# Later row-number conversion, gathered products at 0.9 a block, later gate turning and query sums in one region, in a decoder layer on one Trainium2 core

## The chip, the cores and the metric

The kernel runs on one core of a Trainium2 chip. Five engines work side by side, each through its own list of instructions in order: TensorE (PE: matmuls and transposes), VectorE (DVE), ScalarE (ACT), GpSimd (POOL) and SyncE (SP). SP issues the direct loads, POOL the indirect ones (gathers) and small copies; 16 DMA engines carry them. The metric is the device time of one execution in microseconds; lower is better.

## The reference, cut to what matters

One decoder layer for 256 tokens of width 2048: a mixing part (attention and retention, not touched here) and then a retrieval of experts. For each token and each of 8 heads, 16 of 16384 experts are chosen by two-part keys; each expert is one row of `w_u` and one row of `w_v`.

```python
q = (hf @ w_q).reshape(T, PEER_HEADS, 2, PEER_QUERY_DIM // 2)
s_half = jnp.einsum('thpd,hpkd->thpk', q, sub_keys)
v_half, i_half = lax.top_k(s_half, K)                       # K = 16
cand_s = (v_half[:, :, 0, :, None] + v_half[:, :, 1, None, :]).reshape(T, PEER_HEADS, K * K)
cand_i = (i_half[:, :, 0, :, None] * PEER_N_KEYS + i_half[:, :, 1, None, :]).reshape(T, PEER_HEADS, K * K)
top_s, pick = lax.top_k(cand_s, K)
experts = jnp.take_along_axis(cand_i, pick, axis=-1)
gates = jax.nn.softmax(top_s, axis=-1)
...
a = jnp.einsum('cd,ced->ce', hc, w_u[ec])
coef = gc * jax.nn.gelu(a)
return jnp.einsum('ce,ced->cd', coef, w_v[ec])
```

All of it is float32.

## The kernel before, in words

After the mixing part come the **queries**: 16 chunks of `wq`, each a sum over 16 blocks of the input (`t_block`, L232 to L246) into a PSUM tile `psA`. Both operands are split into a high and a low fp32r part, and three products are summed: high by high, high by low, low by high. `psA` has two regions of 256 columns; per block one matmul of 512 columns writes both, one of 256 adds to the second, and `summed` (L249 to L252) adds the regions with a copy on ACT and an addition on DVE.

Then the experts are worked through in **four stages** of 64 blocks each. In the two u stages (`u_half`, called u0 and u1) a block is one 1-MB load of `in_u` on SP and 16 fp32 matmuls (two rows each in the trace, `psU<-xT,raw`) that give the inner products of 128 experts with the dense tokens; in the two v stages (`v_group`, v0 and v1) a block is one 1-MB load of `in_v` and 20 matmuls into `acc`. Loads go into a ring of eight buffers (`set_ring`).

Dense are only 192 of the 256 tokens (TD). The other tokens' experts, and some rows of the last dense ones, are fetched one by one: 176 **gathered products**, each an indirect DMA of 128 rows of 8 KB (1.05 MB) that POOL issues (`gather`, L834) and one DVE instruction over 128x2048 (L942 or L948). They are of four kinds in this order: 32 "m", 64 "u", 16 "o", 64 "v". Up to four gathers are issued ahead of their products (`fetch`, `most`). The row numbers that a gather reads come from the top-k: `rows_of` and `rows_of_o` lay them out by small DMAs on POOL (`sx`, `sm_`, and by way of `dro` the tile `smo`), and two DVE instructions convert them to integers (`off`, `offm`). `STEPS` lists the blocks of v0, u1 and v1 that take a product; in u0 a rule does it (below).

The **gates** of u0's dense tokens are computed inside u0, for each half of the tokens (tt = 1 first, then 0): `cands` and eight `pick` (top-k; three of tt = 1 are done earlier), `gates` (subtract the maximum, for tt = 1 also start and convert the row numbers), `gates_exp` (ACT), `gates_norm` (DVE), `gates_turned` (PE: two transposes into the tile `ptr`, first of the expert numbers `ex`, then of the gates `gt`), `gates_by_slots` (DVE). After both come 24 groups in turn: `g_make` (DVE builds one-hot sets `o`, `o2m`), `g_sum` (PE, tile `pg`), `g_put` (DVE).

Where these stand between the blocks is **planned** when the program is built: `u_half` keeps two estimated clocks, `pe[0]` (a block costs PASS: 4.36 us in u0, 3.93 in u1) and `dve[0]` (each step has a cost: `cands` 4.0, a `pick` 3.9, a product 2.4 to 2.7), and places a step when its engine's clock allows. A transposition is placed once `pe[0]` has reached the chain's `ready` + 4. A product is placed from the third block after the first `fetch`, one a block, while DVE isn't too far ahead. A group's sum is placed once `pe[0]` has passed the estimated end of its one-hots, and only one set may be ahead of the sums. From block 3 on, the order so planned is the program order on PE, DVE and ACT (`fixed`, `pin`). `later` holds steps that `tick()` runs one per block. In u1, when the last "u" product is placed, `o_rows` issues the DMA that brings `h2o` back for the "o" products, and no product is placed for two blocks (`hold`).

Of the kernel before, what the change touches and what calls it, by code (L numbers as in the profile page):

```python
# [20 lines left out]
P = 128  # L21
# [21 lines left out]

STEPS = dict(u0=[j for j in range(6, HALF - 6) if j % 8 != 1], v0=[j for j in range(HALF - 6) if j % 5 != 4],
             u1=[j for j in range(HALF - 10) if j % 5 != 1])

# [4 lines left out]
TUS = (TU, TU - NO)  # L51
PASS = (4.36, 3.93)
NL = 3

# [65 lines left out]
def body(ctx, tc, a, out, dbg=None, stop=None):  # L120
# [112 lines left out]
    def t_blocks(pool, src_chunks, tags=("A", "A"), parts=2, dst=None):  # L233

        if dst:
            split_to(load(src_chunks[0]), *dst, parts)
        w = [dst] if dst else [split(load(c), parts=parts) for c in src_chunks]
        ps = [pool.tile([P, 2, S], F32, name="psA", tag=t) for _, t in zip(w, tags)]
        for k in range(KB):
            sl = slice(k * P, (k + 1) * P)  # L240
            for p_, (hi, lo) in zip(ps, w):
                nc.tensor.matmul(p_, hi[:, sl], act[:, k], start=k == 0, stop=False, skip_group_check=True)  # L242
                nc.tensor.matmul(p_[:, 1, :], lo[:, sl], hh[:, k, :], start=False, stop=k == KB - 1, skip_group_check=True)  # L243
        return ps

    def t_block(pool, src_chunk, tag="A", **kw):  # L246
        return t_blocks(pool, [src_chunk], (tag,), **kw)[0]

    def summed(ps, dst, n=S):  # L249

        nc.scalar.copy(dst, ps[:, 1, 0:n])
        nc.vector.tensor_add(dst, dst, ps[:, 0, 0:n])  # L252

# [498 lines left out]
    with ExitStack() as gctx:  # L752
# [541 lines left out]
        for i in range(16):  # L1294
            ps = first[i] if i < 2 else t_block(up, wq(i), qbank(i), dst=early if i == 2 else None)
            q = tk.tile([P, S], F32, name="pq", bufs=3)
            summed(ps, q)
            pend.append((i, q))
            if i < KB - LATE:
                ada_chunk(5, LATE + i, crow2)  # L1300
            if 4 <= i < 8:
                rows_in(i - 4)
            if i > 1:
                scores(*pend.pop(0))
            if i == 10:
                cands(1, 0, 4)
            elif i in EARLY:
                pick(1, EARLY.index(i))
# [27 lines left out]
        def gates(tt):  # L1336
# [6 lines left out]
            if tt == 1:  # L1343
                vec.tensor_copy(off, sx[:, 0, :])
                vec.tensor_copy(offm, sm_[:, 0, :])
                rows_of_o(0, ex)
                at_[0] = True

# [52 lines left out]
        def u_half(pool, hf, s2):  # L1401
# [4 lines left out]
            pe = [0.0]  # L1406
            dve = [0.0 if hf else 18.0]
            chains = [] if hf else [chain(1), chain(0)]
# [3 lines left out]
            for j in range(HALF):  # L1412
# [6 lines left out]
                def run(c, kinds):  # L1419
                    while c and c[0][0] in kinds:  # L1420
# [8 lines left out]
                        else:  # L1429
                            if pe[0] < c.ready + 4:  # L1430
                                return
# [11 lines left out]
                if summed_ and summed_[0][0] < j:  # L1443
# [3 lines left out]
                    dve[0] += 0.1 + 0.012 * j  # L1447
                if made and made[0][0] < pe[0]:
                    _, q, o = made.pop(0)
                    summed_.append((j, q, g_sum(pool, *o)))  # L1450
                    end += 0.5
# [3 lines left out]
                nxt = order[0] if order else None  # L1455
                if not any(chains) and nxt is not None and not made and dve[0] < end and (not hf or TD // 8 - len(order) < 1 + 0.45 * j):
                    if not oh:
# [25 lines left out]
                else:  # L1483
                    if at_[0] and not gone:
                        gone = j
                        fetch()
                    go = gone and j >= gone + 3 and dve[0] < end + (8 if any(chains) else 2) and j < HALF - 5
                if go and left[0]:
                    sparse(1)
                    dve[0] += 2.7 if any(chains) else 2.4  # L1490
# [60 lines left out]
```

## Time and profile before

| | us |
|---|---|
| median of 3 runs (lowest, highest) | 1874.88 (1872.93, 1877.63) |
| profiled execution, its own time | 1876.13 |
| its span | 1874.4 |
| PE busy | 1781.3 (95%) |
| DVE busy | 1532.1 (82%) |
| matmuls of u0 and u1 (`psU`) | 551.3 |
| queries, from about | 566 to 665 |
| u0, from about | 660 to 993 |
| v0, from about | 993 to 1286 |
| u1, from about | 1286 to 1561 |

Busy is the time in which an engine executes; PE is busy nearly throughout, so its few idle stretches and what ends them are what to look for. In the rows of a timeline, "[7.36 <-DVE gt L818]" says that the engine sat idle 7.36 us before the instruction, until DVE's write of `gt` released it. L818 is the line of a helper through which all planned instructions of DVE, ACT and PE are recorded, so those rows are told apart by their tiles. `sm__5028` is `sm_` or its integer copy, `s`, `raw` and `rows` as outputs of L834 are the buffers that gathers fill.

### The profile page before, as it was taken

Reading aid. Unit: us, or ns where it says so; the run is one execution under the profiler, and the core shown is the slowest. Engines: PE = TensorE matmul, PEld = TensorE weight load, DVE = VectorE, ACT = ScalarE, POOL = GpSimd, SP = SyncE. Lnnn points to the kernel's source line nnn. Section 1 sums busy time; section 2 is a strip of 40 time slices with the busy share of each in tenths; the row PEclk is TensorE's granted clock in tenths of the full one; section 3 lists DMA queues with packets and bytes.
Section 4 is the critical chain, followed back from the end, with each engine's and each line's share of the span. In section 5 each row is a group of like instructions: output and inputs, shape, how many; then the busy total and the mean of one; then the engine's idle time right before and its main releaser. Section 6 shows DMA issues by size and latency. Waiting matters only on the chain.

```text
span 1874.4 us, 28635 instructions
## 1 busy us (share of the span) xinstructions
PE 1781.3 (95%) x11296; PEld 1558.8 (83%) x11296; DVE 1532.1 (82%) x2378; ACT 707.9 (38%) x1281; POOL 425.2 (23%) x289
## 2 busy tenths in 40 slices
PE   5899999999889998979999999999899999999996
PEld 4899888798668898979998777778899998777774
DVE  7988889899689996679978999974667736999887
ACT  3444454645344421011124554552111114555554
POOL 1000001011010023222213544421323214444310
PEclk9999899999899999989999999999899999999998
DMA  8989888889788779999998999998999989999993
GB/s 345 404 324 374 299 299 306 341 301 343 286 318 298 268 258 332 419 426 424 425 387 342 414 417 415 406 330 365 409 426 426 426 366 363 420 420 418 392 333 97
DMA packets 97496, 673.00 MB, mean 359 GB/s; under 512 B 11905, under 2 KB 12177, under 8 KB 19025
## 3 DMA queue, kind: packets, MB, share of 16 engines
q1 hardware_dynamic: 66818, 467.78, 64.3%
q0 software_dynamic: 30544, 203.40, 26.8%
q8 instruction: 89, 1.46, 0.3%
q14 instruction: 45, 0.37, 0.0%
HBM read 662.81 MB, written 5.41 MB: 357 GB/s over the span
## 4 chain that ended last, share of the span: by engine, by line
PE 76%; DMA 10%; DVE 9%; issue 3%; ACT 1%; POOL 1%; SPq 0%; POOLq 0%; ACTq 0%; DVEq 0%
PE acc L1090 30%; PE psU L818 21%; PE psN L458 7%; PE psA L242 3%; PE bkB L359 2%; PE psD L359 2%; DMA raw<-in_adaT 2%; DMA rows<-in_urow,sm__5028 2%; DVE wlo L162 2%; DVE raw L202 2%; PE psA L243 2%; PE pg L818 1%; PE bkC L359 1%; PE bvB L411 1%; DMA raw<-in_v 1%
## 5 line engine op out<-in xcount | busy, mean ns | idle before, releaser
L818 PE MATMUL psU<-xT,raw 128*128 128x160 f32 (+1 forms) x4096 | 551.3, 296 | 0.0
L818 PEld LDWEIGHTS psU<-xT,raw 128*128 128x128 f32 x4096 | 540.0, 192 | 0.2
L1090 PE MATMUL acc<-whi,cc 128*128 128x512 f32 x1512 | 369.4, 391 | 0.0
L1067 DVE TENSOR_TENSOR wlo<-raw,whi 128x2048 fp32r<-128x2048 f32 x126 | 287.9, 2285 | 67.5 <-issue 50.9
L1090 PEld LDWEIGHTS acc<-whi,cc 128*128 128x128 f32 x1512 | 283.9, 188 | 70.3 <-issue 1.9
L1090 PE MATMUL acc<-wlo,cc 128*128 128x512 f32 x1008 | 253.8, 392 | 0.0
L1064 ACT CAST whi<-raw 128x2048 fp32r<-128x2048 f32 x126 | 240.8, 1912 | 3.4 <-DMA raw<-in_v 3.4
L202 DVE SCALAR_TENSOR_TENSOR raw<-raw,crow 128x2048 f32<-128x2048 f32 x96 | 218.9, 2282 | 21.3 <-DMA raw<-in_adaT 21.2
L161 ACT CAST whi<-raw 128x1024 fp32r<-128x1024 f32 (+1 forms) x174 | 168.5, 1019 | 167.9 <-PE psN L458 34.8
L162 DVE TENSOR_TENSOR wlo<-raw,whi 128x1024 fp32r<-128x1024 f32 (+1 forms) x174 | 200.4, 1179 | 23.8 <-ACT whi L161 23.3
L1090 PEld LDWEIGHTS acc<-wlo,cc 128*128 128x128 f32 x1008 | 162.3, 161 | 61.1 <-issue 0.8
L458 PE MATMUL psN<-whi,act 128*128 128x512 f32 x512 | 167.9, 404 | 1.4 <-ACT act L682 0.7
L818 ACT ACTIVATE X<-psU 128x160 f32<-128x160 f32 (+18 forms) x96 | 24.7, 258 | 309.6 <-PE psU L818 309.6
L1053 ACT CAST cc<-X 128x192 fp32r<-128x192 f32 x126 | 44.1, 353 | 222.5 <-PE acc L1090 222.2
L458 PEld LDWEIGHTS psN<-whi,act 128*128 128x128 f32 x512 | 96.6, 191 | 25.9 <-issue 1.7
L458 PE MATMUL psN<-wlo,act 128*128 128x512 f32 x256 | 104.4, 408 | 6.6 <-DVE wlo L162 6.6
L818 DVE TENSOR_TENSOR X<-X,ge 128x144 f32<-128x144 f32 (+19 forms) x93 | 24.3, 263 | 98.4 <-ACT ge L818 98.1
L834 POOL DMA_INDIRECT rows<-in_v,sx x31 | 71.2, 2297 | 140.7 <-DVE sp L948 64.7
L834 POOL DMA_INDIRECT rows<-in_urow,sx x31 | 77.9, 2514 | 101.7 <-DVE rows L942 85.8
L834 POOL DMA_INDIRECT s<-in_urow,sx x29 | 62.2, 2144 | 157.0 <-DVE s L942 110.3
L242 PE MATMUL psA<-act,whi 128*128 128x512 f32 x240 | 87.3, 405 | 3.8 <-ACT whi L161 3.8
L834 POOL DMA_INDIRECT xT<-in_v,sx x22 | 60.8, 2763 | 101.7 <-DVE sp L948 65.8
(385 smaller groups left out, 2618.9 us busy)
## 6 DMA issues: line engine op xcount, KB each, us to landing
raw<-in_u SPq DMA_DIRECT2D x128, 1024.0 KB, 11.9
raw<-in_v SPq DMA_DIRECT2D x128, 1024.0 KB, 10.2
raw<-in_adaT SPq DMA_DIRECT2D x96, 1024.0 KB, 6.7
raw<-in_winN SPq DMA_DIRECT2D x16, 1024.0 KB, 6.9
raw<-in_woutN SPq DMA_DIRECT2D x16, 1024.0 KB, 6.5
raw<-in_wqT SPq DMA_DIRECT2D x16, 1024.0 KB, 6.0
raw<-in_winB SPq DMA_DIRECT2D x16, 832.0 KB, 6.5
raw<-in_winD SPq DMA_DIRECT2D x12, 1024.0 KB, 6.9
```

What stands on the lines that cost most here:

```text
L161: nc.scalar.copy(hi[:, sl], r[:, sl])
L162: nc.vector.tensor_sub(lo[:, sl], r[:, sl], hi[:, sl].bitcast(F32))
L202: nc.vector.scalar_tensor_tensor(r, r, 1.0, crow, op0=OP.mult, op1=OP.mult, accum_out=modc[:, j, k:k + 1])
L242: nc.tensor.matmul(p_, hi[:, sl], act[:, k], start=k == 0, stop=False, skip_group_check=True)
L359: nc.tensor.matmul(bank[:, b, :], x[:, w], y[:, k, :], start=k == k0 and n == 0 and first, stop=k == k1 - 1 and n == 2, skip_group_check=True)
L458: nc.tensor.matmul(ps[tt], x[:, k, ts_], y[:, w], start=k == 0 and j == 0, stop=k == KB - 1 and j == 2)
L818: i = f(*a, **k)
L834: pin(nc.gpsimd.indirect_dma_start(out=r, out_offset=None, in_=src, in_offset=bass.IndirectOffsetOnAxis(ap=o, axis=0)))
L1053: inorder(nc.scalar.copy(ch, xb(j)))
L1064: inorder(nc.scalar.copy(hi, r))
L1067: nc.vector.tensor_sub(lo[:, i:i + n], r[:, i:i + n], hi[:, i:i + n].bitcast(F32))
L1090: return nc.tensor.matmul(acc[c][0:m], x, w[:, c[1] * 512:(c[1] + 1) * 512], start=jj == 0 and n == 0, stop=jj == HALF - 1 and n == 2 - c[ ...
```

## The change: what it does

1. `t_blocks`: `psA` is one region of 256 columns; per block three matmuls of 256 columns add into it. `summed` is gone, one ACT copy takes its place.
2. `gates(1)`: the two conversions no longer stand right behind the subtraction; they run four ticks later. The first `fetch` follows them, three blocks later than before by the plan (block 11 for block 8), and the first product is at block 14 for 11.
3. u0's products: `taken < RATE * (j - gone - 2)` with RATE 0.9 in place of one a block.
4. A transposition waits for `ready` + 9 in place of + 4; the estimated DVE clock of u1 starts at 4.0 in place of 0; a sum is placed only when `pe[0]` has passed the end of its one-hots by 2; two sets may be ahead of the sums for groups below TUS.
5. `STEPS`: v0 takes a product in five of six blocks in place of four of five; u1 in five of six up to block 57, in place of four of five up to block 53.

By the plan u0 takes 41 products (48 before), v0 49 (47), u1 46 (41), v1 40 (40).

```diff
-STEPS = dict(u0=[j for j in range(6, HALF - 6) if j % 8 != 1], v0=[j for j in range(HALF - 6) if j % 5 != 4],
-             u1=[j for j in range(HALF - 10) if j % 5 != 1])
+STEPS = dict(u0=[j for j in range(6, HALF - 6) if j % 8 != 1], v0=[j for j in range(HALF - 6) if j % 6 != 5],
+             u1=[j for j in range(HALF - 6) if j % 6 != 1])
...
+RATE = 0.9
...
-        ps = [pool.tile([P, 2, S], F32, name="psA", tag=t) for _, t in zip(w, tags)]
+        ps = [pool.tile([P, S], F32, name="psA", tag=t) for _, t in zip(w, tags)]
...
-                nc.tensor.matmul(p_, hi[:, sl], act[:, k], start=k == 0, stop=False, skip_group_check=True)
-                nc.tensor.matmul(p_[:, 1, :], lo[:, sl], hh[:, k, :], start=False, stop=k == KB - 1, skip_group_check=True)
+                for n, (x, y) in enumerate(((hi, hh), (hi, hl), (lo, hh))):
+                    nc.tensor.matmul(p_, x[:, sl], y[:, k, :], start=k == 0 and n == 0, stop=k == KB - 1 and n == 2)
...
-            summed(ps, q)
+            nc.scalar.copy(q, ps)
...
             if tt == 1:
-                vec.tensor_copy(off, sx[:, 0, :])
-                vec.tensor_copy(offm, sm_[:, 0, :])
                 rows_of_o(0, ex)
-                at_[0] = True
+
+                def convert():
+                    vec.tensor_copy(offm, sm_[:, 0, :])
+                    vec.tensor_copy(off, sx[:, 0, :])
+                    at_[0] = True
+                later.append([lambda: None] * 3 + [convert])
...
-            dve = [0.0 if hf else 18.0]
+            dve = [4.0 if hf else 18.0]
+            taken = 0
...
-                            if pe[0] < c.ready + 4:
+                            if pe[0] < c.ready + 9:
...
-                if made and made[0][0] < pe[0]:
+                if made and made[0][0] + 2 < pe[0]:
...
-                if not any(chains) and nxt is not None and not made and dve[0] < end and (...):
+                if not any(chains) and nxt is not None and len(made) < 1 + (8 * nxt < TUS[hf]) and dve[0] < end and (...):
...
-                    go = gone and j >= gone + 3 and dve[0] < end + (8 if any(chains) else 2) and j < HALF - 5
+                    go = gone and taken < RATE * (j - gone - 2) and dve[0] < end + (8 if any(chains) else 2) and j < HALF - 5
                 if go and left[0]:
+                    taken += 1
```

What moves on the engines, in the lists of both programs (the lines of the changed program lie four lower: L814 for L818). First DVE in u0, where the row numbers of tt = 1 are converted. Before, behind the last `pick` (its last row writes `ex`) and the copy of rows into `sx`:

```order
L818 TENSOR_REDUCE ex<-eqc 128x16
L1315 COPY sx<-ex 64x64
L818 CAST sx<-sx 128x64
L818 CAST sm__5028<-sm__5028 128x32
L818 CAST idf<-I_0_5044 128x256
L818 TENSOR_SCALAR idf<-idf 128x8x16
L818 TENSOR_TENSOR cs<-V_0_5042 128x8x16
```

Now, behind the third `pick` of tt = 0, with the normalising of tt = 1 right after:

```order
L814 TENSOR_TENSOR eqc<-eqh,ce 128x800
L814 TENSOR_REDUCE ex<-eqc 128x16
L814 CAST sm__5028<-sm__5028 128x32
L814 CAST sx<-sx 128x64
L814 TENSOR_REDUCE sm<-gt 128x8
L814 RECIPROCAL sm<-sm 128x8
L814 TENSOR_SCALAR sm<-sm 128x8
L814 TENSOR_TENSOR gt<-gt,sm 128x128
```

The two casts have moved behind the candidates (`idf`, `cs`) and three picks of the other half, and the first is now that of `sm_`.

PE in u0, from the blocks ahead of the first `ptr` to the first `pg` (32 rows of `psU` are a block). Before:

```order
L818 MATMUL psU<-xT,raw 128x160 x64
L818 MATMUL ptr<-ident_5018,ex 128x128
L818 MATMUL ptr<-ident_5018,gt 128x128
L818 MATMUL psU<-xT,raw 128x160 x304
L818 MATMUL ptr<-ident_5018,ex 128x128
L818 MATMUL ptr<-ident_5018,gt 128x128
L818 MATMUL psU<-xT,raw 128x160 x32
L818 LDWEIGHTS o_7176
L818 MATMUL pg<-o_7178,o_7176 128x64
```

Now:

```order
L814 MATMUL psU<-xT,raw 128x160 x112
L814 MATMUL ptr<-ident_5018,ex 128x128
L814 MATMUL ptr<-ident_5018,gt 128x128
L814 MATMUL psU<-xT,raw 128x160 x224
L814 MATMUL ptr<-ident_5018,ex 128x128
L814 MATMUL ptr<-ident_5018,gt 128x128
L814 MATMUL psU<-xT,raw 128x160 x48
L814 LDWEIGHTS o_7361
L814 MATMUL pg<-o_7363,o_7361 128x64
```

The list counts a matmul of a block once, so 16 are a block there: the first pair of transposes stands three blocks later than before, five blocks fewer lie between the two pairs, and three blocks for two between the second pair and the first slot sum.

POOL from the last layout of `sx` to the first gather. Before:

```order
L1314 DMA sx<-ex 64x64
L1321 DMA sm__5028<-ex 32x32
L859 DMA h2od<-raw 16x2048 x8
L1321 DMA sm__5028<-ex 32x32
L1328 DMA dro<-ex 16x8x16
L1329 DMA smo<-dro 128x16
L834 DMA s_6158<-in_urow,sm__5028 128x2048
```

Now:

```order
L1310 DMA sx<-ex 64x64
L843 DMA h2m<-h2m 32x512 x3
L1317 DMA sm__5028<-ex 32x32 x2
L1324 DMA dro<-ex 16x8x16
L855 DMA h2od<-raw 16x2048 x8
L1325 DMA smo<-dro 128x16
L830 DMA s_6398<-in_urow,sm__5028 128x2048
```

The eight copies to `h2od` have moved behind the row pieces and `dro`; the gathers stand behind all of it in both. The list of SP is the same in both.

DVE in u1, ahead of the first "o" product. Before, from the last "u" product (`h2t`) at block 0 on:

```order
L942 SCALAR_TENSOR_TENSOR rows,dots<-rows,h2t 128x2048
L818 TENSOR_TENSOR dots<-dots,sx 128x64
L818 TENSOR_TENSOR X_6152<-X_6152,pg 128x8x2
L818 TENSOR_TENSOR X_6152<-X_6152,ge 128x8
L818 TENSOR_TENSOR X_6152<-X_6152,pg 128x8x3
L818 TENSOR_TENSOR o_10903<-iota_5020,idx 128x1024
L818 TENSOR_TENSOR eq<-iota_5020,idx 128x512
L818 TENSOR_TENSOR o_10905<-eq,gat 128x512 x2
L942 SCALAR_TENSOR_TENSOR rows,doto<-rows,h2o 128x2048
```

Now the last "u" product stands at block 6, and these rows at blocks 8 and 9:

```order
L814 TENSOR_TENSOR X_6392<-X_6392,pg 128x8x8
L814 TENSOR_TENSOR X_6392<-X_6392,ge 128x32
L814 TENSOR_TENSOR o_11354<-iota_5020,idx 128x1024
L814 TENSOR_TENSOR eq<-iota_5020,idx 128x512
L814 TENSOR_TENSOR o_11356<-eq,gat 128x512 x2
L938 SCALAR_TENSOR_TENSOR raw,doto<-raw,h2o 128x2048
```

The first "o" product (`h2o`) has moved from block 3 to block 9, and the DMA that brings `h2o` with the last "u" product, from block 0 to block 6.

More of the change, by code (lines that the diff above doesn't have):

```diff
@@ L247, in t_block @@
         return t_blocks(pool, [src_chunk], (tag,), **kw)[0]
-    def summed(ps, dst, n=S):
-        nc.scalar.copy(dst, ps[:, 1, 0:n])
-        nc.vector.tensor_add(dst, dst, ps[:, 0, 0:n])
     def sumsq(wpool, kb, acc, src, tag="pr"):
@@ L1455, in u_half @@
                 nxt = order[0] if order else None
-                if not any(chains) and nxt is not None and not made and dve[0] < end and (not hf or TD // 8 - len(order) < 1 + 0.45 * j):
+                if not any(chains) and nxt is not None and len(made) < 1 + (8 * nxt < TUS[hf]) and dve[0] < end and (not hf or TD // 8 - len(order) < 1 + 0.45 * j):
                     if not oh:
```

## The prediction

> **What bounds it now.** First the page's head and its chain of waits, then windows by stage.
>
> ```profile
> span 1874.4 us, 28635 instructions
> PE 76%; DMA 10%; DVE 9%; issue 3%; ACT 1%; POOL 1%; SPq 0%; POOLq 0%; ACTq 0%; DVEq 0%
> ```
>
> The chain that ended last is mostly PE, so the time goes where PE idles. The windows (columns: stretch, length, busy us of PE, PEld, DVE, ACT, POOL, granted clock, DMA share, GB/s) say where that is:
>
> ```profile
> 566.00:665.00 99.00, 99.00 (x584) 87.27 (x585) 95.35 (x297) 40.48 (x62) 2.10 (x4) 0.98 0.81 292
> 720.00:835.00 115.00, 96.87 (x676) 96.41 (x677) 83.13 (x167) 9.89 (x26) 29.80 (x30) 0.91 1.00 414
> 835.00:965.00 130.00, 129.85 (x1231) 128.96 (x1230) 120.86 (x224) 18.88 (x84) 32.13 (x28) 1.00 1.01 424
> 965.00:995.00 30.00, 27.19 (x224) 26.43 (x221) 20.27 (x35) 11.98 (x26) 3.70 (x3) 0.94 0.85 321
> 1215.00:1275.00 60.00, 60.00 (x264) 46.42 (x263) 46.02 (x38) 30.21 (x40) 14.16 (x6) 1.00 0.83 305
> 1275.00:1530.00 255.00, 248.76 (x2278) 245.20 (x2276) 159.52 (x255) 42.22 (x168) 66.27 (x43) 0.98 1.01 421
> ```
>
> The queries (566 to 665) and the first v stage's end (1215 to 1275) have no idle PE. The first u stage (u0) loses 18 us in 720 to 835 and 2.8 at its end, the second (u1) 6.2. In most of these stretches the DMA share is full, at 414 to 424 GB/s: a 1.0486 MB transfer, one load or one gather, costs 1.0486/0.424 = 2.47 us of it. u0's PE timeline (start, duration, matmuls; idle before and its releaser) has the losses singly:
>
> ```profile
> 700.34 17.55 PE L818 MATMUL psU<-xT,raw 128*128 128x160 f32 x128
> 717.73 0.27 PE L818 MATMUL ptr<-ident,ex 128*128 128x128 f32 x1
> 725.37 0.48 PE L818 MATMUL ptr<-ident,gt 128*128 128x128 f32 x1 [7.36 <-DVE gt L818]
> 725.64 84.71 PE L818 MATMUL psU<-xT,raw 128*128 128x160 f32 x608
> 810.18 0.27 PE L818 MATMUL ptr<-ident,ex 128*128 128x128 f32 x1
> 823.07 0.48 PE L818 MATMUL ptr<-ident,gt 128*128 128x128 f32 x1 [12.61 <-DVE gt L818]
> 823.34 11.45 PE L818 MATMUL psU<-xT,raw 128*128 128x160 f32 x64
> 834.93 0.94 PE L818 MATMUL pg<-o,o 128*128 128x64 f16 x16
> 981.66 0.52 PE L818 MATMUL pg<-o2m,o1m 128*128 128x64 bf16 x2 [2.53 <-DVE o2m L818]
> 983.47 9.98 PE L818 MATMUL psU<-xT,raw 128*128 128x160 f32 x64
> ```
>
> Twice the second transposition of a token half's gates waits for the normalised gates, and once a slot sum (pg) for its one-hots: 7.36 + 12.61 + 2.53 = 22.5 us. The undisturbed pace is (717.73 - 700.34)/128 = 0.1359 us a matmul row, 4.35 a block of 32. After the waits it is slower: 608 took 84.54 to the next ptr (82.6 at the pace, 1.9 lost), 64 took 11.59 (2.9 lost), 64 took 9.98 (1.2 lost against half of the 17.55): 6.0 us. So 28.5 us hang on three waits. A rule on those 6.0: the Trainium skill (TensorE: Matmul & The Clock Gate, What's actually happening) has the clock fall to half after an idle window of about 3.4 us and return after as long busy. By it the 2.53-us wait might cost no clock, and 4.8 of the 6.0 would be won; the row shows 1.2 lost there, and the row decides.
>
> Why DVE was late, from its timeline and POOL's:
>
> ```profile
> 717.35 0.18 DVE L818 CAST sm__5028<-sm__5028 128x32 int32<-128x32 f32 x1 [13.04 <-DMA sm__5028<-ex]
> 745.14 0.56 POOL L1329 DMA_DIRECT2D smo<-dro  x1 [14.89 <-DMA dro<-gt]
> 780.44 2.29 DVE L942 SCALAR_TENSOR_TENSOR raw<-raw,h2m 128x2048 f32<-128x2048 f32 x1 [1.23 <-DMA raw<-in_urow,sm__5028]
> 805.03 2.29 DVE L942 SCALAR_TENSOR_TENSOR s<-s,h2m 128x2048 f32<-128x2048 f32 x1 [1.25 <-DMA s<-in_urow,sm__5028]
> 814.88 2.29 DVE L942 SCALAR_TENSOR_TENSOR s<-s,h2m 128x2048 f32<-128x2048 f32 x1 [2.63 <-DMA s<-in_urow,sm__5028]
> 819.75 2.29 DVE L942 SCALAR_TENSOR_TENSOR raw<-raw,h2m 128x2048 f32<-128x2048 f32 x1 [2.57 <-DMA raw<-in_urow,sm__5028]
> 824.67 2.29 DVE L942 SCALAR_TENSOR_TENSOR s<-s,h2m 128x2048 f32<-128x2048 f32 x1 [1.66 <-DMA s<-in_urow,sm__5028]
> ```
>
> DVE stood 13.04 us at the conversion of the row numbers; everything behind it in DVE's order, the first normalising included, came that much late. Later each product waits for its gather, and they arrive every 4.9 us (814.88, 819.75, 824.67), which is two transfers of 2.47: loads and gathers take turns. The order wanted one product per 4.35-us block, so DVE fell behind until the second ptr stood 12.61 us.
>
> **The change, part by part.**
>
> *Conversion three blocks later.* The 13.04-us wait goes if the row DMAs have landed by then. Between the gates' subtraction and the conversion now stand the second half's candidates and three picks; the planner's own costs are 4.0 + 3 x 3.9 = 15.7 us, more than 13.04. On POOL the last two row pieces stand ahead of the eight h2od copies instead of among and behind them, so they land rather sooner. The normalising follows the conversion, and ptr comes three blocks (13 us) later: its 7.36 us goes, I take all of it (between 7.36 and a rest of 3). SP's order is unchanged. DVE reaches the conversion at about 717.35 - 13.04 + 15.7 = 720, so the first four gathers, which wait for it on POOL, start within some 3 us of before. Behind them on POOL smo still waits for dro (14.89 us before), and gather 5 behind that, as before.
>
> *0.9 products a block.* 48 products planned in u0 become 41; u0's spacing is 4.35/0.9 = 4.83 us against arrivals of 4.9, so DVE keeps nearly level. The second normalising is now behind product 10 (before: 780.44; now 776 to 780 as an estimate) with ptr at an estimated 791, three to four blocks later instead of one. 12.61 goes. First one-hots then stand at an estimated 802, first pg at 804, with two makes allowed ahead of the sums: a margin of 2 us or less, where an arrival late by 4 would be seen. I take 1.5 of new wait (0 to 4 by the arrival spacing; the nearest rows, waits of 1.2 to 2.6 at products, sit at its middle). The end's 2.53 has two makes of cover and goes. u0: -28.5 + 1.5 = -27.0.
>
> *The seven products moved.* The first v stage takes 49 for 47 at five of six blocks, u1 46 for 41, the last v stage 40 as before. In the v stage PE has no idle and the DMA share falls to 0.83 at its end, so two gathers (4.9 us of transfer) fit in 60 x 0.17 = 10 us free; they cost 0 (up to 3 if DVE at five products per six blocks falls behind; not below 0, as nothing is taken out).
>
> *u1.* Its rows (PE; DVE; then the SP issue of one load and its landing; PE):
>
> ```profile
> 1303.05 8.09 PE L818 MATMUL psU<-xT,raw 128*128 128x144 f32 x64
> 1311.01 2.29 DVE L942 SCALAR_TENSOR_TENSOR rows<-rows,h2o 128x2048 f32<-128x2048 f32 x1 [9.77 <-DMA h2o<-h2od]
> 1317.28 1.29 PE L818 MATMUL pg<-o,o 128*128 128x64 f16 x16 [6.14 <-DVE o L818]
> 1318.38 10.60 PE L818 MATMUL psU<-xT,raw 128*128 128x144 f32 x64
> 1484.09 0.33 SPq L152 DMA_DIRECT2D raw<-in_u  x1
> DMA to landing us min/median/max: 23.1/23.1/23.1
> 1509.68 10.54 PE L818 MATMUL psU<-xT,raw 128*128 128x144 f32 x84
> ```
>
> DVE waits 9.77 us for the h2o rows and makes PE wait 6.14, then 64 matmuls take 10.60 for 8.09: 8.6 us in all. Now the last u product is at block 6, the h2o load goes out there, and the first o product stands at block 9 behind a one-hot set that PE needs only at block 14; those five blocks hide a wait of 10. The 8.6 goes. What is late next: the loads of u. The one issued at 1484.09 lands at 1507.2; block 51 starts at 1509.68 and its 32 rows end 10.54 x 32/84 = 4.0 later, so the load had 6.5 us to spare. The DMA is full (421 GB/s over 1275 to 1530). Without the 8.6 us PE asks for it that much earlier, and by that block two more gathers (4.9) share the queue: 8.6 + 4.9 - 6.5 = 7.0 us short, new PE waits for loads. Bounds: 0 if the first v stage hands over loads earlier, 19 if every block went at the five-in-six pace (rival below); I take the row. u1: -8.6 + 7.0 = -1.6.
>
> *Query sums.* Per k, one 512-column and one 256-column matmul become three of 256:
>
> ```profile
> L242 PE MATMUL psA<-act,whi 128*128 128x512 f32 x240 | 87.3, 405 | 3.8 <-ACT whi L161 3.8
> 89.34 22.76 PE bkC L359 x192
> L252 DVE TENSOR_TENSOR pq<-pq,psA 128x256 f32<-128x256 f32 x15 | 6.0, 406 | 3.4 <-ACT pq L251 3.4
> ```
>
> In the projection, 192 256-column matmuls take 22.76 us, 0.1185 each; three are 0.355, and the 512 with its 256 comes to 0.353 by the same count of columns. 256 times 0.002 is +0.5 us. The removed adds (0.406 each, 16 of them) are worth nothing: PE is busy for 99.00 of 99.00 us there and hides them. Were DVE the limit, 6.5 us would be won; it is at 95.35, so I keep +0.5 (range -3 to +3).
>
> Sum against the profiled execution (1876.13 us for a span of 1874.4): -27.0 - 1.6 + 0.5 = -28.1, or 1848.0; that execution is 1.25 above the median of 1874.88, so 1847.
>
> **The rivals.**
> - *All three stalls gone and DMA room in u1*: no 1.5, no 7.0, so 1838. For it: the share falls to 0.83 at 1215 to 1275, room to load ahead. The Trainium skill (DMA: Bandwidth & Descriptors, Where 436 GB/s comes from) has a ceiling of 435 GB/s; at that a transfer would be 2.41 us and the shortage some 2 us less. The trace stays at 424. Chance 0.11.
> - *The wait comes back at u0's first slot sum*, gathers 10 us later than estimated, DVE with them: +10, 1857. For it: the margin there is 2 us, and smo's 14.89. Against: 0.9 a block holds level. Chance 0.13.
> - *u1 paced by the DMA throughout*: five gathers in six blocks and one load per block is 1.833 x 2.47 = 4.53 us a block, against 8.09/2 = 4.05. With some 0.15 of slot sums a block (an estimate from the 0.94 us of the row at 834.93, 24 sums in 64 blocks, their ends overlapping) PE is 0.33 faster; over 58 blocks that is 19 us of waits for the 7, 1859. For it: the row's 23.1 us to land. Against: before, four in five (4.45) left 6.5 us over at block 52, so loads held ahead cover a part. Chance 0.08.
> - *Slower: the waits return as load waits.* u0 gets 27 us shorter at an already full DMA, so it passes 27/2.47 = 11 transfers less; seven are gathers, four are loads' lead, and all must pass later. If the later stages have no room, PE waits out the 27 us in u1, block by block. Each wait there costs slow clock, 1.2 to 2.9 us by the rows above, 2 in the middle; eight waits of 3.4 us cost 16, against 6.0 + 2.5 saved: 1875 + 7.5 = 1883. It decides once 965 to 995 and 1215 to 1275 can't be filled beyond 0.85 and 0.83, which hold 15 us. Against: with no gather queued these rates are what PE asked for, and three other windows hold 414 to 424. Chance 0.05.
> - *No change: the bytes set the end.*
>
> ```profile
> HBM read 662.81 MB, written 5.41 MB: 357 GB/s over the span
> ```
>
> Were this mean all that memory gives, removed waits would move nothing: 1875. The 424 GB/s over 130 us speaks against it. Chance 0.03. The Trainium skill (DMA: Bandwidth & Descriptors, Specifications) speaks for it: it limits a core to about 358 GB/s from HBM. By that rule no wait removed would shorten the span; the trace disagrees in every stretch with gathers.
>
> **How the numbers follow.** The forecast, 1847 (1840 to 1854 by its own bounds), has 0.60. The first rival lies at 1838, the second and third at 1857 and 1859. A range of 1836 to 1862 holds these four, 0.92 less the spread at their ends, say 0.84. A measurement tells this kernel from no change at about 0.3%, 5.6 us. Faster: 0.60 + 0.11 + 0.13 + 0.08 = 0.92, less 0.01 for mishaps not named; same 0.04; slower 0.05.
>
> **What would show it.** Right: no PE idle over 3 us at either ptr, none at the u1 pg; the conversion with a wait under 2 us; waits of PE for u loads, 3 to 10 us in sum, after block 40 of u1; the queries within 1 us of before. Wrong: a conversion that still waits for its DMA (then the first term fails), a wait of over 5 us at u0's first pg (the second), loads late already in u0 (the DMA term, since u0 too has 1.9 transfers, 4.7 us, to 4.35 us of PE and lives on its margin), or PE idle in the first v stage.

## The result, and the profile after

The changed kernel takes 1853.95 us (median of 4 runs, 1850.65 to 1858.14) against 1874.26 (4 runs): a ratio of 0.989, interval 0.9866 to 0.9915, 20 us less. Its profiled execution had 1850.65 us. The forecast was 1847, range 1836 to 1862.

The page of the changed kernel, its head and its chain of waits:

```profile
span 1848.9 us, 29124 instructions
PE 70%; DMA 12%; DVE 10%; issue 5%; ACT 1%; POOL 1%; SPq 0%; ACTq 0%; POOLq 0%; DVEq 0%
```

Less of the chain is PE now. Its windows (the columns as before), by stage; u1 begins at 1258:

```profile
566.00:665.00 99.00, 98.71 (x832) 98.33 (x832) 93.97 (x305) 39.68 (x62) 2.62 (x5) 1.00 0.79 290
720.00:835.00 115.00, 111.97 (x895) 111.36 (x895) 81.82 (x155) 14.06 (x44) 20.72 (x22) 1.00 1.01 425
835.00:965.00 130.00, 130.00 (x1201) 129.32 (x1199) 106.19 (x197) 25.06 (x86) 24.64 (x23) 1.00 0.98 403
1200.00:1258.00 58.00, 57.54 (x252) 44.16 (x251) 44.87 (x40) 26.00 (x36) 15.60 (x7) 1.00 0.81 308
1258.00:1370.00 112.00, 111.75 (x1048) 111.28 (x1049) 71.80 (x122) 17.78 (x81) 24.89 (x22) 1.00 1.01 426
1370.00:1500.00 130.00, 122.98 (x1147) 120.86 (x1146) 86.77 (x132) 20.42 (x80) 24.38 (x21) 0.99 1.01 426
```

PE idles 3 us in 720 to 835 where it idled 18, and the last window of u0 has none. New is the last row: in the middle of u1 PE idles 7 us, with the DMA full at 426 GB/s. The rows of u0 that answer to the three waits (DVE's conversion, second normalising and first one-hots; then PE's two pairs of transposes and first slot sums):

```profile
711.54 0.17 DVE L814 CAST sm__5028<-sm__5028 128x32 int32<-128x32 f32 x1
781.42 0.28 DVE L814 TENSOR_REDUCE sm<-gt 128x8 f32<-128x128 f32 x1
803.12 0.69 DVE L814 TENSOR_TENSOR o<-iota,idx 128x1024 f16<-128x1024 f16 x1
729.71 0.27 PE L814 MATMUL ptr<-ident,gt 128*128 128x128 f32 x1
790.78 0.27 PE L814 MATMUL ptr<-ident,gt 128*128 128x128 f32 x1
804.66 0.93 PE L814 MATMUL pg<-o,o 128*128 128x64 f16 x16 [0.56 <-DVE o L814]
817.24 0.63 PE L814 MATMUL pg<-o,o 128*128 128x64 f16 x16 [2.32 <-ACT X L814]
```

The conversion waits for nothing, neither transposition waits, the first slot sum waits 0.56 us. What it costs in u1, by DVE's waits, PE's waits, one load of u with its landing, and PE's timeline:

```profile
DVE raw L938 <- DMA h2o<-h2od: 7.0, 1, 7.0
PE psU L814 <- DMA raw<-in_u: 6.3, 8, 2.2
1337.75 0.33 SPq L153 DMA_DIRECT2D raw<-in_u  x1
DMA to landing us min/median/max: 29.1/29.1/29.1
1367.02 4.16 PE L814 MATMUL psU<-xT,raw 128*128 128x144 f32 x32 [0.22 <-DMA raw<-in_u]
1378.34 5.83 PE L814 MATMUL psU<-xT,raw 128*128 128x144 f32 x32 [2.20 <-DMA raw<-in_u]
```

The h2o wait is still there on DVE, 7.0 us, but no row of PE waits for it. The load for block 26 takes 29.1 us to land, just when PE wants it, and from there to block 50 PE waits eight times for a load. (The loads issued in this u1 take 27.4 us in the median, 13.9 in the kernel before.) The 2.20-us wait makes the next block 5.83 us long for 4.16; the granted clock is 0.50 there from 1379.3 to 1382.7. In all, PE idles 7.2 of u1's 277.1 us, 6.3 of them for loads, and is busy for 269.9.

The stages, from the starts of the first matmuls of each in the timeline, with those of the experiments below (us; "queries" from the first of them to block 4 of u0, "u0" from block 4 on, v1 with all that follows):

| kernel | queries | u0 | v0 | u1 | v1 | median | ratio to before, interval |
|---|---|---|---|---|---|---|---|
| before | 121.5 | 307.2 | 293.1 | 274.4 | 313.7 | 1874.26 | |
| changed | 123.3 | 280.1 | 293.1 | 277.1 | 313.7 | 1853.95 | 0.989 (0.9866 to 0.9915) |
| sums_alone | 123.5 | 303.0 | 293.1 | 274.7 | 313.7 | 1874.08 | 0.9987 (0.9969 to 1.0004) |
| convert_alone | 121.6 | 287.3 | 293.1 | 274.6 | 313.5 | 1856.56 | 0.9908 (0.9877 to 0.9938) |
| convert_at_once | 122.9 | 290.8 | 292.8 | 280.9 | 311.7 | 1865.98 | 0.9948 (0.993 to 0.9966) |
| rate_one | 122.9 | 288.2 | 293.1 | 277.2 | 315.3 | 1865.52 | 0.9943 (0.9925 to 0.9961) |
| turn_at_four | 123.4 | 277.1 | 293.1 | 277.1 | 313.7 | 1851.19 | 0.9872 (0.9847 to 0.9898) |
| old_sums | 122.0 | 284.0 | 293.1 | 277.3 | 315.6 | 1860.36 | 0.9913 (0.9897 to 0.9929) |
| u1_old_pace | 122.9 | 280.0 | 293.1 | 273.2 | 323.3 | 1856.97 | 0.9905 (0.9889 to 0.9921) |
| u1_two_thirds | 123.5 | 279.7 | 293.1 | 265.5 | 325.6 | 1854.87 | 0.9894 (0.9877 to 0.9911) |
| shift4 | 123.3 | 280.1 | 293.1 | 289.4 | 315.8 | 1868.52 | 0.9954 (0.9938 to 0.997) |
| best2 | 122.9 | 277.4 | 294.1 | 290.0 | 316.0 | 1864.86 | 0.9936 (0.9912 to 0.9959) |
| best3 | 123.1 | 278.0 | 293.1 | 270.9 | 313.8 | 1843.14 | 0.9818 (0.9803 to 0.9833) |

The stages are from one profiled execution each; the median carries what differs ahead of the queries too: their first matmul starts at 560.9 to 573.9 us in these thirteen executions, though nothing of that part is changed (564.5 before, 561.5 in the changed kernel). So differences of a few us are read from the stages. (The expectation for rate_one counts u0 from its first block, which makes 300.3 us of the 280.1.)

### The profile page after: what moved, and what is told of

It reads as the page before. It is cut to its first block, busy times and chain, and to the rows that moved or that the text cites. A ratio compares the mean times of both kernels' runs of the same rounds, so it can differ in the third digit from the quotient of the medians.

```text
span 1848.9 us, 29124 instructions
## 1 busy us (share of the span) xinstructions
PE 1775.5 (96%) x11552; PEld 1564.9 (85%) x11552; DVE 1527.2 (83%) x2358; ACT 706.3 (38%) x1278; POOL 402.9 (22%) x289
## 4 chain that ended last, share of the span: by engine, by line
PE 70%; DMA 12%; DVE 10%; issue 5%; ACT 1%; POOL 1%; SPq 0%; ACTq 0%; POOLq 0%; DVEq 0%
PE acc L1086 30%; PE psU L814 17%; PE psN L454 6%; DMA raw<-in_u 5%; PE psA L244 4%; DMA s<-in_urow,sm__5028 3%; DMA raw<-in_adaT 3%; PE psD L355 3%; PE bkB L355 2%; DVE wlo L163 2%; DVE raw L203 2%; PE bkC L355 1%; PE bvB L407 1%; PE pg L814 1%; DMA raw<-in_winA 1%
## 5 line engine op out<-in xcount | busy, mean ns | idle before, releaser
L814 PE MATMUL psU<-xT,raw 128*128 128x160 f32 (+1 forms) x4096 | 547.1, 294 | 7.7 <-DMA raw<-in_u 6.3
L814 PEld LDWEIGHTS psU<-xT,raw 128*128 128x128 f32 x4096 | 533.8, 191 | 10.3 <-ACT ge L814 5.7
L814 ACT ACTIVATE X<-psU 128x160 f32<-128x160 f32 (+18 forms) x91 | 23.7, 261 | 272.9 <-PE psU L814 272.9
L830 POOL DMA_INDIRECT rows<-in_v,sx x32 | 65.8, 2056 | 167.0 <-DVE sp L944 102.0
L244 PE MATMUL psA<-act,whi 128*128 128x256 f32 x480 | 88.3, 286 | 3.4 <-ACT whi L162 3.4
L944 DVE SCALAR_TENSOR_TENSOR sp<-rows,dots,sp 128x2048 f32<-128x2048 f32 x32 | 75.1, 2346 | 17.8 <-DMA rows<-in_v,sx 17.8
L938 DVE SCALAR_TENSOR_TENSOR rows<-rows,h2t 128x2048 f32<-128x2048 f32 x33 | 75.4, 2284 | 5.4 <-DMA rows<-in_urow,sx 5.4
## 6 DMA issues: line engine op xcount, KB each, us to landing
raw<-in_u SPq DMA_DIRECT2D x128, 1024.0 KB, 20.6
```

Source lines behind the costliest of these rows:

```text
L244: nc.tensor.matmul(p_, x[:, sl], y[:, k, :], start=k == 0 and n == 0, stop=k == KB - 1 and n == 2)
L814: i = f(*a, **k)
L830: pin(nc.gpsimd.indirect_dma_start(out=r, out_offset=None, in_=src, in_offset=bass.IndirectOffsetOnAxis(ap=o, axis=0)))
L938: pin(nc.vector.scalar_tensor_tensor(r, r, 1.0, h, op0=OP.mult, op1=OP.mult, accum_out=d[:, e:e + 1]))
```

## Experiments

**What made u0 shorter: the parts one by one.** Conversion deferred alone, on the kernel before (in every diff here "-" is the kernel started from):

```diff
-                vec.tensor_copy(off, sx[:, 0, :])
-                vec.tensor_copy(offm, sm_[:, 0, :])
                 rows_of_o(0, ex)
-                at_[0] = True
+                def convert():
+                    vec.tensor_copy(offm, sm_[:, 0, :])
+                    vec.tensor_copy(off, sx[:, 0, :])
+                    at_[0] = True
+                later.append([lambda: None] * 3 + [convert])
```

> The kernel before with the deferred conversion alone (the two conversions four ticks later; query sums, products one a block, + 4, pace of v0 and u1 as before). By the plan 45 products in u0, the second ptr before block 25, the first slot sum before block 27. Theory (the conversion's wait makes the first stall, the late products the second, and each needs its own edit): the 13-us wait of DVE goes to under 1 and the first ptr waits 0 to 3 for 7.36; the second normalising still stands behind 10 products and PE, two to three blocks earlier in its list, waits 7 to 9 us at the second ptr and 3 to 4 at the first slot sum; u0 from block 4 on takes 292 to 297 us for 307.2. u1 270 to 274. Total 1859 to 1866. Rival (the conversion's wait is what made everything late): no wait over 2 us is left, u0 280 to 284, total 1848 to 1852.

u0 fell to 287.3, below the range: alone, this part wins 20 us of the 27. Its DVE and PE rows (second normalising, second ptr, first slot sum):

```profile
779.96 0.28 DVE L818 TENSOR_REDUCE sm<-gt 128x8 f32<-128x128 f32 x1
781.06 0.33 PE L818 MATMUL ptr<-ident,gt 128*128 128x128 f32 x1 [2.45 <-DVE gt L818]
793.52 1.29 PE L818 MATMUL pg<-o,o 128*128 128x64 f16 x16 [3.43 <-DVE o L818]
```

In the kernel before, the second normalising stands behind 18 products and starts at 821.97; here it stands behind 10 and starts at 779.96. The waits left are 2.45 and 3.43 (and one of 1.34 later), where 7 to 9 and 3 to 4 were expected: the theory is right in kind, its first price too high.

The other way round, the changed kernel with the conversions where they were (`convert()` called at once in place of `later.append(...)`):

> The changed kernel with the conversions back behind the subtraction, all else as changed: by the plan 44 products in u0, first ptr before block 16, second before block 32, first slot sum before block 35. Theory: DVE waits 10 to 14 us for the row numbers again, the first ptr stands late enough to wait 0 to 3, but 17 products stand ahead of the second normalising for 10, each 4.9 us late: PE waits 6 to 9 us at the second ptr and 2 to 5 at the first slot sum; u0 from block 4 on 288 to 293 us for 280.1, total 1860 to 1868. Rival (later turning alone hides it): u0 within 2 us of the changed kernel, 1852 to 1856.

```profile
703.87 0.24 DVE L814 CAST sm__5028<-sm__5028 128x32 int32<-128x32 f32 x1 [4.17 <-DMA sm__5028<-ex]
816.16 0.47 PE L814 MATMUL ptr<-ident,gt 128*128 128x128 f32 x1 [5.41 <-DVE gt L814]
833.44 0.93 PE L814 MATMUL pg<-o,o 128*128 128x64 f16 x16 [1.31 <-DVE o L814]
```

u0 takes 290.8, in the range: +10.7. But DVE waits only 4.17 us for the row numbers, not 10 to 14, and 17 products stand ahead of the second normalising for 10. So here the deferral helps more by the number of products that it keeps behind the normalising than by the wait that it removes. u1 takes 280.9 in this run because PE stands 10.75 us at a slot sum there, behind the h2o rows:

```profile
1310.99 1.29 PE L814 MATMUL pg<-o,o 128*128 128x64 f16 x16 [10.75 <-DVE o L814]
```

The next kernel shows where the other 9 us of DVE's wait went: the query sums alone, on the kernel before.

```diff
-        ps = [pool.tile([P, 2, S], F32, name="psA", tag=t) for _, t in zip(w, tags)]
+        ps = [pool.tile([P, S], F32, name="psA", tag=t) for _, t in zip(w, tags)]
...
-            summed(ps, q)
+            nc.scalar.copy(q, ps)
```

> The kernel before with the query sums alone changed (one region, three matmuls of 256 columns, no additions). Theory: DVE comes about 4 us earlier to the conversion, but there it waits for the row numbers, whose DMAs go by POOL's order and not by DVE: the wait grows from 13 to 15 to 18 us, queries up to block 4 take 121.5 to 123.5 us, u0 from block 4 on 305 to 309 for 307.2. Total within 3 us of before. Rival (the additions delay the whole chain of gates): u0 4 us shorter, total 1869 to 1872.

Its rows: the last row piece and the copies of h2od on POOL, the conversion on DVE, the second ptr on PE; then, for comparison, the same two of POOL in the kernel before:

```profile
697.00 0.50 POOL L1321 DMA_DIRECT2D sm__5028<-ex  x1 [7.66 <-DVE sx L1315]
699.87 3.83 POOL L859 DMA_DIRECT2D h2od<-raw  x8 [1.84 <-ACT raw L818]
701.22 0.18 DVE L818 CAST sm__5028<-sm__5028 128x32 int32<-128x32 f32 x1 [4.06 <-DMA sm__5028<-ex]
818.57 0.47 PE L818 MATMUL ptr<-ident,gt 128*128 128x128 f32 x1 [19.30 <-DVE gt L818]
```

```profile
701.41 3.83 POOL L859 DMA_DIRECT2D h2od<-raw  x8 [4.95 <-ACT raw L818]
708.89 0.51 POOL L1321 DMA_DIRECT2D sm__5028<-ex  x1 [3.65 <-DMA h2od<-raw]
```

The theory missed. The rival's 4 us in u0 came, but the time of the additions is not all of it. Without the additions the program's order on POOL differs: the last row piece goes out at 697.00 ahead of the h2od copies, not at 708.89 behind them, and the conversion waits 4.06 us for 13.04. The first ptr wait (7.36) is gone. But the second grows from 12.61 to 19.30: as many products (18) stand ahead of the second normalising, which comes only 3 us earlier after block 4 (133.0 us for 136.0), while PE, not held at the first ptr, reaches the second ptr 9.7 us earlier. u0 gains 4.2, the queries lose 2.0, and in the median (1874.08 beside 1878.47 on the same chip) no difference is clear. A wait removed early came back later on the same path.

The changed kernel with the old sums (two regions, copy and addition):

> The changed kernel with the query sums as before: two regions of psA, a 512-column and a 256-column matmul per block of the input, one copy and one addition per chunk. Theory: PE's columns are the same, and the additions of DVE (16 x 0.41 us) are hidden: within 2 us of the changed kernel, rather 0.5 to 1.8 faster. Rival: the additions on DVE, 95 of 99 us busy there, were in the way, and the first blocks of u0 and the top-k then come 3 to 6 us later: 1857 to 1860.

```profile
813.77 1.29 PE L814 MATMUL pg<-o,o 128*128 128x64 f16 x16 [4.12 <-DVE o L814]
```

Queries 1.3 shorter, as the theory said, but u0 3.9 longer: the first slot sum waits 4.12 us for 0.56. DVE reaches the conversion 154.3 us after the first query matmul in place of 150.0. The total, 1860.36, is about the rival's. So the additions were hidden from PE in the queries, and not from DVE, which carries its lateness to the first place where PE waits for it.

The rate, on the changed kernel:

```diff
-RATE = 0.9
+RATE = 1.0
```

> The changed kernel with RATE 1.0 for 0.9: 45 products in u0 for 41, 36 in v1 for 40. Theory (products arrive every 4.9 us, and a block takes 4.35): one product more stands ahead of the second normalising and of the first one-hot set, each 4.9 us late, so PE waits 4 to 6 us at the first slot sum of u0 or the second transposition, and loses 1 to 2 us of clock; u0 takes 305 to 308 us for 300.3. The loads of u0 lose the lead of four gathers, 10 of 11.6 us, so v0 and u1 begin with less; u1 3 to 6 us longer. Total 1862 to 1868. Rival (0.9 is not needed once conversion and turning are later): u0 within 1 us of the changed kernel and the total at 1850 to 1855.

```profile
813.02 1.30 PE L814 MATMUL pg<-o,o 128*128 128x64 f16 x16 [4.52 <-DVE o L814]
907.00 0.63 PE L814 MATMUL pg<-o,o 128*128 128x64 f16 x16 [3.06 <-ACT X L814]
1301.59 1.01 PE L814 MATMUL pg<-o,o 128*128 128x64 f16 x16 [10.14 <-ACT X L814]
```

One product more ahead makes the first slot sum wait 4.52 us, and three later sums wait 4.3 us for ACT: u0 288.2, +8.1, a little over the range. That u1 is as long as in the changed kernel (277.2) is chance: no row of PE waits for a load there, but a slot sum waits 10.14 us (last row), while DVE stands 13.15 us for the h2o rows. Whether the loads begin u1 with less lead, this run does not show.

The margin of the turning, on the changed kernel:

```diff
-                            if pe[0] < c.ready + 9:
+                            if pe[0] < c.ready + 4:
```

> The changed kernel with ready + 4 for + 9 before a transposition: ptr before blocks 11 and 26 for 14 and 28, first slot sum before block 29 for 31, two products fewer ahead of the first one-hots. Theory (the order of DVE behind the conversion is what counts, the margin of the turning not): the first normalising ends 1 us before block 11, the second within 1 us of block 26, so PE waits 0 to 2 us at each ptr, and 0 to 2 at the first slot sum; u0 278 to 283 us for 280.1, total within 4 us of the changed kernel. Rival (the later turning removes the ptr waits): 5 to 10 us of wait at the two ptr, u0 287 to 293.

```profile
779.34 0.28 DVE L814 TENSOR_REDUCE sm<-gt 128x8 f32<-128x128 f32 x1
791.36 0.69 DVE L814 TENSOR_TENSOR o<-iota,idx 128x1024 f16<-128x1024 f16 x1
781.96 0.27 PE L814 MATMUL ptr<-ident,gt 128*128 128x128 f32 x1
```

No ptr waits, and u0 takes 277.1, 3.0 less than in the changed kernel. With the rest of the change in place the later turning buys nothing. It moves two more products ahead of the first one-hots, which start at 803.12 with it and at 791.36 without. The other parts of points 4 and 5 (the 2 us behind the one-hots, two sets ahead, v0's pace) were not tried one by one.

**What made u1 longer: loads, or something else?** Fewer gathers in u1, first with the list of the kernel before (u1_old_pace):

```diff
-             u1=[j for j in range(HALF - 6) if j % 6 != 1])
+             u1=[j for j in range(HALF - 10) if j % 5 != 1])
```

> The changed kernel with u1's list of product blocks as before (four in five up to block 53): 41 products in u1 and 45 in v1 by the plan. Theory (u1 is bound by the DMA, and the lead of the loads is used up from block 25 on): by block 50 the old list has placed only one product less, so 2.5 us of transfer are relieved there and the four left out later stand where the loads already have a lead again; u1 274 to 275 us for 277.1, and v1, with 45 products for 40 in its 51 blocks, 0 to 4 us longer: 1852 to 1856, no difference that counts. Rival (the pace of five in six is what costs u1 its 11 us): u1 back at 268 or less, total 1845.

then with two of three blocks (u1_two_thirds):

```diff
-             u1=[j for j in range(HALF - 6) if j % 6 != 1])
+             u1=[j for j in range(HALF - 6) if j % 3 != 1])
```

> The changed kernel with a product in two of three blocks of u1: 39 in u1 and 47 in v1 by the plan, and six gathers less than in the changed kernel up to block 50. Theory (DMA-bound u1): 6 x 2.47 = 15 us less to transfer before the point where the waits end, more than the 11 us lost, so u1 takes 266 to 268 us for 277.1, with no wait of PE for a load of u over 0.5 us. v1's DVE, busy 94 of 100 us at 40 products, has to take 47: 3 to 10 us longer. Together 1846 to 1854. Rival (u1 loses its time to something else, such as ACT or the slot sums): u1 stays at 275 to 277 and the total rises to 1857 to 1863.

Windows of u1 with two thirds:

```profile
1260.00:1372.00 112.00, 111.52 (x1049) 111.18 (x1049) 67.25 (x118) 19.53 (x84) 17.45 (x19) 1.00 1.01 426
1372.00:1502.00 130.00, 130.00 (x1238) 129.71 (x1238) 81.37 (x134) 20.61 (x81) 21.28 (x19) 1.00 1.01 424
```

With six gathers less by block 50 u1 takes 265.5 us, 11.6 less, no PE row waits for a load, and the 7 us of idle are gone: u1's loss in the changed kernel is the transfer of loads and gathers together. Of the 11.6 us, 7.2 are idle time and 4.4 are longer matmuls (PE busy 269.9 for 265.5), of which the half clock behind the 2.20-us wait makes half of 3.4, 1.7; the rest was not followed. With the old pace u1 takes 273.2, near the expected 274, but not as the theory had it: no row of PE waits for a load, and a slot sum waits 5.07 us behind the h2o rows instead. That wait gives the loads time too, so this run does not tell the pace from the wait. v1 pays more than expected both times, 9.6 and 11.9 us for 5 and 7 products more. With two thirds the last product starts here on DVE, 289 us into v1:

```profile
1814.97 2.35 DVE L944 SCALAR_TENSOR_TENSOR sp<-xT,dots,sp 128x2048 f32<-128x2048 f32 x1 [1.22 <-DMA xT<-in_v,sx]
```

In the changed kernel it is this one, 258 us into v1:

```profile
1792.86 2.34 DVE L944 SCALAR_TENSOR_TENSOR sp<-xT,dots,sp 128x2048 f32<-128x2048 f32 x1
```

The final additions need that sum, so they all come late.

**A version that beats both.** Products go from u1 to u0 and v0:

```diff
-... v0=[j for j in range(HALF - 6) if j % 6 != 5],
-             u1=[j for j in range(HALF - 6) if j % 6 != 1])
+... v0=[j for j in range(HALF - 3) if j % 6 != 5],
+             u1=[j for j in range(HALF - 6) if j % 6 != 1 and j % 9 != 5])
...
-                    go = gone and taken < RATE * (j - gone - 2) and ...
+                    go = gone and taken < RATE * (j - gone - 2) + max(0, j - 38) * 0.15 and ...
```

> A version meant to beat the changed kernel: products moved out of u1 to where DMA has room. By the plan 43 products in u0 (two more, from block 38 on), 51 in v0 (blocks 58 and 60 too), 40 in u1 (thinned evenly, five less up to block 50), 42 in v1. Theory (u1 DMA-bound, v1 bound by DVE at its end): u1 266 to 269 us for 277.1; u0 and v0 0 to 2 us longer, living on the loads' lead of 11.6 us at u0's end and on the free share of DMA at v0's end; v1 and the tail 2 to 4 us longer. Total 1846 to 1851. Rival: the loads' lead at u1's start is smaller by what v0's end now carries, so u1 stays at 273 or more and the total at 1853 to 1858.

u0 and v0 carried four products more at no cost (280.1, 293.1), but u1 took 289.4. Its rows (POOL's issue of h2o, DVE's first o product, PE's slot sum):

```profile
1280.20 0.57 POOL L861 DMA_DIRECT2D h2o<-h2od  x1 [3.88 <-DVE raw L938]
1297.26 2.29 DVE L938 SCALAR_TENSOR_TENSOR rows<-rows,h2o 128x2048 f32<-128x2048 f32 x1 [15.63 <-DMA h2o<-h2od]
1300.87 1.01 PE L814 MATMUL pg<-o,o 128*128 128x64 f16 x16 [22.37 <-ACT X L814]
```

With 82 products left at u1's start for 86, the last u product stands at block 2 of the plan and the first o product one block behind it, and the h2o load takes 17.0 us to land (in the changed kernel too). Next, ready + 4 and a longer pause, with u0 and v0 as in shift4 and the changed kernel's list in u1:

```diff
-                    hold = 2
+                    hold = 5
```

> A second version meant to beat the changed kernel: ready + 4, as in the run with that margin; 43 products in u0 and 50 to 51 in v0 as in shift4; u1 with the changed kernel's list, but no o product for five blocks after a step of the sparse part ends, in place of two: by the plan 41 products in u1, four less up to block 50, 41 in v1. Theory (the 22-us stall of shift4 is the h2o load, 16 us on its way when the first o product stands two blocks behind it; u1's loads recover with four gathers less): no wait over 2 us at u1's slot sums, u1 266 to 270 us, u0 from block 4 on 277 to 279, v0 293, v1 and the tail 314 to 316 together: 1840 to 1844 where the changed kernel has 1849 to 1854. Rival (the stall is not the h2o load but the thinned u1 list or the load ring): a wait of 10 to 20 us stays at u1's first sums, 1853 to 1863.

The same wait stayed, 15.62 us on DVE and 22.4 on PE, u1 290.0. The edit did not do what it was meant to do, so it decides nothing between theory and rival. The pause starts when the sparse steps' list ends, and by then the o product of block 3 had been placed. So the pause has to start with the product:

```diff
                     sparse(1)
+                    if hf and left[0] == NS + NO:
+                        hold = 7
...
-                    hold = 2
+                    hold = max(hold, 2)
```

> As the version before it (ready + 4, 43 products in u0, 50 to 51 in v0), but the pause now starts with the last u product itself and lasts seven blocks; before, the list of the sparse steps ended a block too late and the first o product still stood one block behind the last u product. By the plan u1 places its first o product at block 9, 42 products in u1, four less than the changed kernel up to block 50, 40 in v1. Theory (the stall is the h2o load, 16 us on its way; u1's other loss is DMA): DVE waits 0 to 3 us for h2o, PE waits at no slot sum of u1, 0 to 3 us for loads; u1 266 to 270 us, u0 from block 4 on 277 to 278, v0 293 to 294, v1 and tail 313 to 316: 1838 to 1844. Rival (loads short as in the changed kernel because v0's end now carries gathers): u1 273 to 277, 1846 to 1852.

No row of DVE waits for h2o, and none of PE for a load; windows of its u1:

```profile
1268.00:1380.00 112.00, 108.08 (x1008) 107.68 (x1009) 66.50 (x115) 18.28 (x79) 21.90 (x21) 0.98 1.01 426
1380.00:1510.00 130.00, 130.00 (x1239) 129.71 (x1238) 84.39 (x132) 21.34 (x84) 23.41 (x20) 1.00 1.01 426
```

u1 270.9 (a wait of 3.9 at one slot sum for ACT is left), v0 and v1 as they were: 1843.14 us, 0.9818 (0.9803 to 0.9833) of the time before, about 11 us below the changed kernel, 8 by the stages. With the pause moved the 22-us wait is gone, so it was the h2o load; that the loads keep up can also be due to the 3.9 us. Its profiled execution alone had 1854.53 us: its first query matmul started at 573.9, the latest of all.

## Why the prediction was right, and where its steps were not

- *u0, -27.0*: measured 307.2 to 280.1, -27.1. The second normalising was estimated for 776 to 780, the second ptr for 791, the first one-hots for 802 and the first sum for 804; they came at 781.42, 790.67, 803.12 and 804.66. That the number fits to 0.1 is partly luck: the new waits are 0.56 and 2.32, 2.9 us for the 1.5 taken, and some 1.5 us were won elsewhere in u0. The share of the parts was wrong. The conversion's wait was put down to the deferral, but sums_alone and convert_at_once show that most of it (13.04 to about 4) goes already with the order on POOL that comes with the new query sums; the deferral without that order (convert_alone) removes it too. What the deferral does beyond that is to leave 10 products ahead of the second normalising for 17 or 18. The "later" turning was counted as part of the gain; it costs 3.0. Undone singly in the changed kernel, deferral, rate and query sums cost 10.7, 8.1 and 3.9 us of u0; added singly to the kernel before, deferral wins 19.9 and the sums 4.2. The parts overlap, so such shares don't add up.
- *u1, -1.6*: measured +2.7. That the 8.6 us go and that loads fall short in their place held, and the 7.0 us of new load waits are 6.3 in the rows. The sum missed what came with them: PE is busy 4.4 us longer than in u1_two_thirds, 1.7 of it at half clock behind the 2.20-us wait (the rest was not followed), and waits 0.9 us for ACT. Slower matmuls behind a wait the prediction had counted for the old waits and left out for the new ones.
- *u1, the place of its load waits*: it was wrong too. The 6.5 us were the margin at block 52, the smallest in the kernel before, and the waits begin at block 26. The load for block 25 lands 16.0 us before its first matmul in the kernel before and 0.6 in the changed one, because PE's wait of 6.14 us at the slot sum, before block 26, also gave the loads time. convert_at_once shows this: it has the changed kernel's list in u1 and 23 gathers issued by block 26 for 20, but PE stands 10.75 us at a slot sum, and the load for block 25 lands 13.6 us early (at block 5, ahead of that stand, the leads are 15.9 and 12.4); one load wait of 0.86 us is left. That the 6.3 us are transfers is shown by u1_two_thirds. That the h2o wait is hidden hangs on the counts of this plan: with one part undone it is back (10.75, 10.14 and 5.07 us of PE in convert_at_once, rate_one and u1_old_pace).
- *Query sums, +0.5*: measured +1.8 in the changed kernel and, undone, -1.3. The 0.353 us for a 512- and a 256-column matmul stands in no row shown, and what makes the 1.8 was not followed. The removed additions were priced at nothing because PE hid them. They were worth 3.9 us in u0: the cover named was PE's, and the engine to ask was DVE, which is late at the first slot sum. For the same reason DVE came to the conversion 150.0 us after the first query matmul, not the 155.5 that lie in "about 720".
- *Moved products, 0*: v0 took 293.1 in both, v1 313.7 in both.
- *Sum*: -27.1 + 1.8 + 2.7 = -22.6 by the stages for -28.1; another 3.0 of the profiled executions' difference lie ahead of the queries. The medians differ by 20.3. So the time came out inside the range but 7 us above the forecast, and most of the 5.5 us that the stages miss is u1's 4.3.
- *Signs named*: no wait at either ptr, none at u1's slot sums, a conversion without a wait, and 6.3 us of load waits (3 to 10 named) held. Two did not: the load waits begin at block 26, not after 40, and the queries are 1.8 us longer, not within 1.
- *Rivals*: the first, nothing left of the stalls and room in u1, fell with the load waits. A wait at u0's first sum (0.56) came only when one part was undone (4.52, 4.12). The third rival, u1 paced by DMA, is partly what happened: 6.3 us of load waits and 4.4 us of longer matmuls, for its 19. "The waits return as load waits" fell: 6.3 us of load waits came in u1, not 27. The last one, bytes as the limit, fell with the 426 GB/s that hold over u1 from 1258 to 1500. The Trainium skill (DMA: Bandwidth & Descriptors, Specifications) has about 358 GB/s per core from HBM; the trace disagrees for this core.

## What to carry to other kernels

Count what stands ahead of a late step on its engine before counting the wait in front of it: eighteen products ahead of a normalising, each as slow as its transfer, were the stall, and with eight fewer its wait fell from 12.61 to 2.45 us. A wait that goes also gave its neighbours time (loads ran ahead); price the next resource with that time taken away, at the first block where it runs out and not at the last, and with the slower work behind each short wait. When a plan shifts a count by a few, look where every step that depends on that count lands: four products fewer left put a load and its user one block apart; PE stood 22 us there, and u1 became 12 us longer.

## What was not expected of the hardware

- A 1-MB load issued among loads and gathers takes long: the h2o rows 20.7 us in the kernel before and 17.0 in the changed one, and DVE stood 15.6 us for them in two versions. A load of u takes 11.9 us in the median of the kernel before and 20.6 in the changed one.
- A wait of PE of 2.20 us made the following block 1.67 us longer (5.83 for 4.16), and one of 2.53 us in the kernel before the following two blocks 1.2 us. The granted clock is 0.50 in both places, from 1379.3 to 1382.7 here and from 982.2 to 985.6 there, where slot sums filled the first 1.3 us of it. Behind the 2.32-us wait in the changed kernel's u0 it stays at 1.00 (817.2 to 825), so the length of a wait alone does not tell what follows it.
- The part ahead of the queries, the same code in all, ended 13 us apart between executions (560.9 to 573.9), while v0 took 293.1 us in eleven of thirteen.
